# Opening stage of a two-layer diffusion backbone: constant products ahead of the first block, h transferred after the second, transposes and sums at other places

## The chip, the core and the metric

The kernel runs on one core of one Trainium2 chip. The metric is device time in microseconds of one execution, as the median of several. All arithmetic on the tokens is float32 in effect: large products are made of three products in a rounded float32 form, small ones of full float32 products.

## What is computed

The reference is a backbone of two layers over 256 latent and 256 context tokens of 1024 channels. In each layer both token sets pass a half-step gated FFN, then three parallel token mixers (grouped-query attention, differential attention, Fourier mixing) merged by gates, then a second half-step FFN. Every norm is modulated by vectors that come from a conditioning vector:

```python
ml = jnp.split(jax.nn.silu(c) @ w_ada[l] + b_ada[l], N_MOD, axis=-1)
mc = jnp.split(jax.nn.silu(c_ctx)[None] @ w_ada[l] + b_ada[l], N_MOD, axis=-1)
def ffn_half(h, m, k, g_norm, wi, wo):
    hn = modulate(rmsnorm(h, g_norm), m[3 * k], m[3 * k + 1])
    return h + 0.5 * m[3 * k + 2][:, None, :] * swiglu(hn, wi, wo)
```

So the first FFN can start only when three things are there: the first two of nine modulation vectors (shift and scale, 1024 channels each, for c and for c_ctx), the reciprocal root mean square of every token of h, and the first FFN weights.

## The kernel before

**Layout.** Activations lie with channels on the 128 partitions: h is 128 x 8 x 512, eight channel tiles (kt) by 512 tokens (256 latent, 256 context, called the two halves). Weights are held as a high and a low part; a product of activations is three matmuls, `mm3` (lines 309 to 311): high by high, high by low, low by high. The weights come through `WeightStream`: SyncE loads a piece into one of three raw buffers (`wraw`, line 192), ScalarE casts a part of it to the high form (`whi`, line 203), VectorE subtracts to get the low form (`wlo`, line 204), and the next piece is loaded into a raw buffer once both its parts are split.

**The opening, `start`.** The shift and scale of the first norm are made here. Their weights are four blocks `wst[0..3]` of 128 x 8 x 512, 2 MB each: scale and shift of channels 0 to 511 (blocks 0 and 1), then scale and shift of channels 512 to 1023 (blocks 2 and 3). They land in the tiles mg_start, yb_start and, for blocks 2 and 3, two tiles that the profile prints as u_start. SyncE issues everything in written order: `small` (biases, gains, the conditioning vectors), block 0 in five transfers, block 1 in four, with the four transfers of h (512 KB each) between its first and its second half, then blocks 2 and 3, and behind them the first FFN weights.

The steps on the engines, with their lines:

- `dots(i, kts)` (1149): for each channel tile of block i one full float32 product with `scol`, the SiLU of the two conditioning vectors, as stationary operand of two columns and 512 columns of w_ada moving past it. A full float32 product stands in the trace as two MATMUL rows, each with its weight load. The sum over eight channel tiles is copied by ScalarE to `rows` (1151; the profile prints the tile as pt_start).
- `columns(i)` (1157 to 1159): four small transposes turn the two rows into columns, and VectorE adds the bias (line 1159, tile ada).
- squares and sums: ScalarE squares h (1173), VectorE adds the eight channel tiles to one (1171), TensorE sums over the partitions by four products with a column of ones (1186), VectorE takes the reciprocal root (lines 277 to 284) and scales an identity with it (1190), and one product with ones spreads the result over all partitions: r (1195).
- `apply(hf)`: VectorE makes acol, the gain by one plus scale (374); then for each channel tile and half it scales h by acol and r (386), ScalarE adds the shift and rounds to the high part (389), and VectorE makes the low part (390). `apply(0)` covers channel tiles 0 to 3, `apply(1)` 4 to 7. Line 386 needs acol, so the block of scales; lines 389 and 390 need the block of shifts.

Behind `start` comes `cond_region`: GpSimd copies one element of acol (322) as a marker, and behind it loads the conditioning vectors once more, 1 MB (323), for the other modulation vectors, which VectorE forms by multiply and sum during the FFNs (lines 326, 327, 356), with w_ada loaded by GpSimd. The first FFN (`first_pair`) opens with channel tiles 0 to 3 for four accumulators, then tiles 4 to 7.

**What sets the order.** Each engine's order of instructions is settled when the program is built, from the order of the text and from when an operand is reckoned to be ready; so a later step can stand ahead of an earlier one that is not ready. Inside `manual_schedule` for TensorE the matmuls of `start` keep their written order among themselves. In the trace of before, four matmuls of the first FFN stand ahead of the transposes of `columns(3)`.

Of the kernel before, what the change touches and what calls it, by code (L numbers as in the profile page):

```python
# [18 lines left out]
P = 128  # L19
D = 1024  # L20
KT = 8
# [27 lines left out]
def _half(half):  # L49
    return slice(half * 256, half * 256 + 256)  # L50
# [55 lines left out]
class Interleave:  # L106
# [9 lines left out]
    def add(self, q, task, gen=None):  # L116
        if gen is not None:
            task.gen = gen
        self.queues[q].append(task)
        return task  # L120

    def start(self, task, gen):
        task.gen = gen
        self.queues[0].append(task)
        self.step(task)
# [95 lines left out]
class Net:  # L221
# [898 lines left out]
    def start(self):  # L1120

        nc, io = self.nc, self.io
        ccol = self.ccol
        scol = self.pool.tile([P, KT, 2], F32, name="scol")
        nc.sync.dma_start(self.small, io["small"])
        self.h = self.region("h", F32, "start")
        rows = self.region("pt", F32, "start")
        chunks = []
        for i, tag in enumerate(("mg", "yb", "u0", "u1")):
            t = self.region(tag, F32, "start")  # L1130
            for a, b in (((0, 1), (1, 2), (2, 4), (4, 6), (6, 8)) if i == 0 else ((0, 2), (2, 4), (4, 6), (6, 8))):
                nc.sync.dma_start(t[:, a:b, :], io["wst"][i][:, a:b, :])
                if (i, b) == (1, 4):
                    for x in range(4):
                        nc.sync.dma_start(self.h[:, 2 * x:2 * x + 2, :], io["h"][:, 2 * x:2 * x + 2, :])
            chunks.append(t)
        nc.scalar.activation(scol, ccol, AF.Tanh, scale=0.5)
        nc.vector.scalar_tensor_tensor(scol, scol, 1.0, ccol, op0=ALU.add, op1=ALU.mult)
        nc.vector.tensor_scalar(scol, scol, 0.5, None, op0=ALU.mult)
        make_identity(nc, self.ident)  # L1140
        nc.vector.memset(self.ones, 1.0)

        ps = {}

        def dots(i, kts):
            if kts[0] == 0:
                ps[i] = self.mm.next()
            for kt in kts:
                nc.tensor.matmul(ps[i][:2, :], scol[:, kt, :], chunks[i][:, kt, :], start=kt == 0, stop=kt == KT - 1)  # L1149
            if kts[-1] == KT - 1:  # L1150
                nc.scalar.copy(rows[:2, i, :], ps[i][:2, :])

        def columns(i):
            mod, hf = 1 - i % 2, i // 2
            pc = self.mm.next()
            for x in range(4):
                nc.tensor.transpose(pc[:, 2 * x:2 * x + 2], rows[:2, i, x * P:x * P + P], self.ident[:2, :2])
            a = mod * KT + 4 * hf
            nc.vector.tensor_tensor(self.ada[0][:, a:a + 4, :], pc[:, 0:8].rearrange("p (a c) -> p a c", c=2),
                                    self.bada[:, 0, a:a + 4].unsqueeze(2).to_broadcast([P, 4, 2]), op=ALU.add)  # L1160

        def apply(hf):
            ks = slice(4 * hf, 4 * hf + 4)
            self.norm_scale(0, 0, 2, ks)
            for kt in range(ks.start, ks.stop):
                for half in range(2):
                    self.norm_apply(0, 0, kt, half, r[:, _half(half)])

        sq = self.region("ya", F32, "squares")
        two = [sq[:, 2 * i:2 * i + 2, :] for i in range(4)]  # L1170
        add = lambda y, x: nc.vector.tensor_tensor(y, y, x, op=ALU.add)
        for i in range(4):
            nc.scalar.activation(two[i], self.h[:, 2 * i:2 * i + 2, :], AF.Square)
        for y, x in ((0, 1), (2, 3), (0, 2)):
            add(two[y], two[x])
        add(sq[:, 0, :], sq[:, 1, :])
        dg = self.e1.next()
        with self.tc.manual_schedule(engines={mybir.EngineType.PE}):
            dots(0, range(8))
            dots(1, (0, 1))  # L1180
            columns(0)
            dots(1, range(2, 8))
            dots(2, (0,))
            bank = self.att.next()
            for i in range(4):
                nc.tensor.matmul(bank[:, i:i + 1], sq[:, 0, i * P:i * P + P], self.ones[:, 0:1], start=True, stop=True)
            x, y, z = (self.sm.next()[:, 0:4] for _ in range(3))
            self.rsqrt(y, x, bank[:, 0:4], D, z)
            for i in range(4):
                nc.vector.tensor_scalar(dg[:, i * P:i * P + P], self.ident, y[:, i:i + 1], None, op0=ALU.mult)  # L1190
            dots(2, (1,))
            columns(1)
            dots(2, (2, 3, 4))
            r = self.att.next()
            nc.tensor.matmul(r, self.ones, dg, start=True, stop=True)
            apply(0)
            dots(2, (5, 6, 7))
            dots(3, (0, 1))
            columns(2)
            nc.vector.tensor_copy(self.identr, self.ident)  # L1200
            dots(3, range(2, 8))
            columns(3)
            apply(1)
# [141 lines left out]
```

## Time and profile before

| | us |
|---|---|
| median of three runs | 2100.65 |
| lowest and highest | 2099.33, 2103.11 |
| profiled execution | 2100.76 |
| its span, first to last instruction | 2098.7 |
| TensorE matmul busy | 2075.1 (99%) |
| VectorE busy | 1489.6 (71%) |
| ScalarE busy | 920.0 (44%) |
| GpSimd busy | 114.5 (5%) |

The profiled execution is one run; the rows further down are of that run, with times in microseconds from the start of its span. Engines are PE (TensorE matmuls), PEld (its weight loads, which overlap), DVE (VectorE), ACT (ScalarE), POOL (GpSimd) and SP (SyncE, which issues transfers). A busy share is an average over stages; the opening is about 40 of 2100 us. A matmul's printed duration is longer than the distance to the next one, since matmuls overlap at their ends; for what a stretch costs, read the distance between starts.

### The profile page before, as it was taken

The numbers are of one execution on the slowest core, as the hardware profiler recorded it, in microseconds if no ns is written. First come the engines' busy times: TensorE is split into PE (matmuls) and PEld (weight loads), VectorE is DVE, ScalarE is ACT, GpSimd is POOL, SyncE is SP. The second block draws the span as 40 slices with busy tenths as digits, with TensorE's granted clock in tenths as the row PEclk, the third lists the DMA queues.
The fourth block names the chain that finished last, engine by engine and source line by source line (L and its number), as shares of the span: only waits on it lengthen the run. The fifth ranks groups of instructions, "written<-read, shape, count | busy, mean of one in ns | idle before, by whom it ended". The sixth has DMA issues, their size and how long they took to land.

```text
span 2098.7 us, 31520 instructions
## 1 busy us (share of the span) xinstructions
PE 2075.1 (99%) x11640; PEld 1807.9 (86%) x11640; DVE 1489.6 (71%) x3113; ACT 920.0 (44%) x1905; POOL 114.5 (5%) x235
## 2 busy tenths in 40 slices
PE   8999999999999999999999999999999999999999
PEld 3888888899989988988888898888888899999999
DVE  5878776667878865776666668766556688889764
ACT  3323333356765543433333333233334576656553
POOL 2000001100000110000000001000010000000000
PEclk9999999999999999999999999999999999999999
DMA  7645555322222242244444425555553323355665
GB/s 274 229 158 197 174 171 176 98 86 64 70 71 71 86 161 91 74 169 150 153 148 148 143 73 201 181 187 162 179 166 109 96 91 113 122 179 175 197 186 147
DMA packets 86937, 300.47 MB, mean 143 GB/s; under 512 B 10112, under 2 KB 11264, under 8 KB 86528
## 3 DMA queue, kind: packets, MB, share of 16 engines
q1 hardware_dynamic: 64800, 219.29, 32.1%
q0 software_dynamic: 21984, 79.18, 12.1%
q8 instruction: 91, 1.49, 0.3%
q14 instruction: 62, 0.51, 0.1%
HBM read 293.19 MB, written 5.24 MB: 142 GB/s over the span
## 4 chain that ended last, share of the span: by engine, by line
PE 94%; DVE 3%; DMA 2%; ACT 1%; issue 1%; SPq 0%; ACTq 0%; DVEq 0%
PE mm L309 29%; PE mm L311 28%; PE mm L310 28%; PE att L734 1%; PE att L768 1%; PE att L749 1%; DVE wlo L204 1%; PE att L750 1%; PE att L792 1%; PE mm L1149 1%; PE att L311 1%; PE att L310 1%; PE att L309 1%; PE att L303 0%; DMA yb_start<-in_wst 0%
## 5 line engine op out<-in xcount | busy, mean ns | idle before, releaser
L203 ACT CAST whi<-wraw 128x512 fp32r<-128x512 f32 (+2 forms) x840 | 497.9, 596 | 871.1 <-PE mm L310 768.7
L204 DVE TENSOR_TENSOR wlo<-wraw,whi 128x512 fp32r<-128x512 f32 (+2 forms) x840 | 548.8, 658 | 327.5 <-ACT whi L203 323.1
L309 PE MATMUL mm<-hn,whi 128*128 128x512 f32 (+1 forms) x1808 | 641.1, 356 | 1.1 <-ACT hn L389 0.9
L310 PE MATMUL mm<-hn,whi 128*128 128x512 f32 (+1 forms) x1808 | 635.9, 353 | 0.0
L311 PE MATMUL mm<-hn,wlo 128*128 128x512 f32 (+1 forms) x1808 | 635.8, 353 | 0.1
L311 PEld LDWEIGHTS mm<-hn,wlo 128*128 128x128 f32 x1808 | 339.4, 188 | 51.4 <-DVE wlo L204 0.5
L309 PEld LDWEIGHTS mm<-hn,whi 128*128 128x128 f32 x1808 | 339.0, 188 | 49.3 <-issue 1.2
L310 PEld LDWEIGHTS mm<-hn,whi 128*128 128x128 f32 x1808 | 339.3, 188 | 47.4 <-DVE hn L390 0.2
L309 PE MATMUL mm<-whi,hn 128*128 128x384 f32 (+3 forms) x432 | 146.7, 340 | 1.7 <-DVE mg_m L953 1.7
L311 PE MATMUL mm<-whi,hn 128*128 128x384 f32 (+3 forms) x432 | 143.6, 332 | 0.0
L310 PE MATMUL mm<-wlo,hn 128*128 128x384 f32 (+3 forms) x432 | 143.6, 332 | 0.0
L356 DVE CUSTOM_DVE_ANT_0 gt<-ya_c,small 128x1024 bf16<-128x1024 f32 x112 | 141.6, 1280 | 1.7 <-DMA ya_c<-in_wada 1.7
L356 DVE CUSTOM_DVE_ANT_0 e<-ya_c,small 128x1024 bf16<-128x1024 f32 x112 | 141.6, 1280 | 0.0
L352 POOL DMA_DIRECT2D ya_c<-in_wada x128 | 68.1, 532 | 910.9 <-DVE ada L356 882.8
L309 PE MATMUL mm<-u_f,whi 128*128 128x256 f32 (+1 forms) x304 | 101.9, 335 | 0.0
L311 PE MATMUL mm<-u_f,wlo 128*128 128x256 f32 (+1 forms) x304 | 100.9, 332 | 0.0
L310 PE MATMUL mm<-u_f,whi 128*128 128x256 f32 (+1 forms) x304 | 100.9, 332 | 0.0
L438 DVE SCALAR_TENSOR_TENSOR h_h<-mm,gcol,h_h 128x256 f32<-128x256 f32 x104 | 49.9, 482 | 59.9 <-PE mm L311 59.3
L309 PEld LDWEIGHTS mm<-whi,hn 128*128 128x128 f32 x432 | 82.2, 190 | 4.9 <-DVE mg_m L953 2.3
L310 PEld LDWEIGHTS mm<-wlo,hn 128*128 128x128 f32 x432 | 82.3, 191 | 2.5
L311 PEld LDWEIGHTS mm<-whi,hn 128*128 128x128 f32 x432 | 81.9, 190 | 2.7 <-DVE hn L390 0.5
L309 PE MATMUL mm<-mg_f,whi 128*128 128x512 f32 (+1 forms) x204 | 72.1, 353 | 0.0
(288 smaller groups left out, 3284.6 us busy)
## 6 DMA issues: line engine op xcount, KB each, us to landing
wraw<-in_wi SPq DMA_DIRECT2D x172, 512.0 KB, 4.2
ya_c<-in_wada POOLq DMA_DIRECT2D x128, 512.0 KB, 4.0
wraw<-in_wo SPq DMA_DIRECT2D x64, 512.0 KB, 3.7
wraw<-in_gate SPq DMA_DIRECT2D x48, 512.0 KB, 3.6
wraw<-in_win SPq DMA_DIRECT2D x48, 384.0 KB, 3.1
wraw<-in_wo SPq DMA_DIRECT2D x32, 384.0 KB, 3.4
wraw<-in_wbr SPq DMA_DIRECT2D x24, 512.0 KB, 3.5
wraw<-in_wout SPq DMA_DIRECT2D x16, 512.0 KB, 3.6
```

Of the source, the lines that this page charges most:

```text
L203: self.nc.scalar.copy(hi, raw)
L204: self.nc.vector.tensor_tensor(lo, raw, _r(hi), op=ALU.subtract)
L309: mm(out, lh, rh, start=first, stop=False)
L310: mm(out, lh, rl, start=False, stop=False)
L311: mm(out, ll, rh, start=False, stop=last)
L352: self.nc.gpsimd.dma_start(self.adaraw[(self.bg_base + j) % 2], self.io["wada"][l, n])
L356: self.tc.keep_in_program_order(self.nc.vector.tensor_tensor_reduce(self.ft.next().bitcast(BF16), self.adaraw[self.bg_base % 2], self.sil[ ...
L438: self.nc.vector.scalar_tensor_tensor(self.h[:, m, c], ps[:, c], g[:, m, half:half + 1], self.h[:, m, c], op0=ALU.mult, op1=ALU.add)
L734: nc.tensor.matmul(b[:, i * P:i * P + P], src, self.identr, start=True, stop=True)
L749: nc.tensor.matmul(d, qt, k, start=True, stop=False)
L750: nc.tensor.matmul(d, qt, low, start=False, stop=True)
L768: nc.tensor.transpose(ps[:, x * 256 + i * P:x * 256 + i * P + P], es[i][:, k * P:k * P + P], self.ident)
```

## The change

All of it is in `start`. The memset of `ones` stands first in the text. The four transfers of h are issued behind all four of block 1. Ahead of the first dots, TensorE makes eight products of `ones` with `ones` (128 columns) into an otherwise unused accumulator. Among the dots, `columns(0)` follows four channel tiles of block 1 where it followed two; the column sums and the reciprocal root follow four channel tiles of block 2 and `columns(1)` where they followed one channel tile of block 2; `columns(1)` follows four channel tiles of block 2 where it followed two; the spreading product and `apply(0)` follow the whole of block 2 where they followed five channel tiles of it. What stands behind them is unchanged.

```diff
--- before.py
+++ after.py
@@ -1122,6 +1122,7 @@
         nc, io = self.nc, self.io
         ccol = self.ccol
         scol = self.pool.tile([P, KT, 2], F32, name="scol")
+        nc.vector.memset(self.ones, 1.0)
         nc.sync.dma_start(self.small, io["small"])
         self.h = self.region("h", F32, "start")
         rows = self.region("pt", F32, "start")
@@ -1130,7 +1131,7 @@
             t = self.region(tag, F32, "start")
             for a, b in (((0, 1), (1, 2), (2, 4), (4, 6), (6, 8)) if i == 0 else ((0, 2), (2, 4), (4, 6), (6, 8))):
                 nc.sync.dma_start(t[:, a:b, :], io["wst"][i][:, a:b, :])
-                if (i, b) == (1, 4):
+                if (i, b) == (1, KT):
                     for x in range(4):
                         nc.sync.dma_start(self.h[:, 2 * x:2 * x + 2, :], io["h"][:, 2 * x:2 * x + 2, :])
             chunks.append(t)
@@ -1138,7 +1139,6 @@
         nc.vector.scalar_tensor_tensor(scol, scol, 1.0, ccol, op0=ALU.add, op1=ALU.mult)
         nc.vector.tensor_scalar(scol, scol, 0.5, None, op0=ALU.mult)
         make_identity(nc, self.ident)
-        nc.vector.memset(self.ones, 1.0)
 
         ps = {}
 
@@ -1175,12 +1175,17 @@
             add(two[y], two[x])
         add(sq[:, 0, :], sq[:, 1, :])
         dg = self.e1.next()
+        warm = self.att.next()
         with self.tc.manual_schedule(engines={mybir.EngineType.PE}):
+
+            for i in range(8):
+                nc.tensor.matmul(warm[:, 0:P], self.ones, self.ones, start=True, stop=True)
             dots(0, range(8))
-            dots(1, (0, 1))
+            dots(1, range(4))
             columns(0)
-            dots(1, range(2, 8))
-            dots(2, (0,))
+            dots(1, range(4, 8))
+            dots(2, range(4))
+            columns(1)
             bank = self.att.next()
             for i in range(4):
                 nc.tensor.matmul(bank[:, i:i + 1], sq[:, 0, i * P:i * P + P], self.ones[:, 0:1], start=True, stop=True)
@@ -1188,13 +1193,10 @@
             self.rsqrt(y, x, bank[:, 0:4], D, z)
             for i in range(4):
                 nc.vector.tensor_scalar(dg[:, i * P:i * P + P], self.ident, y[:, i:i + 1], None, op0=ALU.mult)
-            dots(2, (1,))
-            columns(1)
-            dots(2, (2, 3, 4))
+            dots(2, range(4, 8))
             r = self.att.next()
             nc.tensor.matmul(r, self.ones, dg, start=True, stop=True)
             apply(0)
-            dots(2, (5, 6, 7))
             dots(3, (0, 1))
             columns(2)
             nc.vector.tensor_copy(self.identr, self.ident)
```

## Rows read from the trace of the kernel before

**Rows 1.** The page, busy time: each engine's us, share of the span, instructions.

```profile
PE 2075.1 (99%) x11640; PEld 1807.9 (86%) x11640; DVE 1489.6 (71%) x3113; ACT 920.0 (44%) x1905; POOL 114.5 (5%) x235
```

**Rows 2.** The chain of waits in order of time, 0 to 62 us: start us, us, what.

```profile
9.53 10.21 DMA yb_start<-in_wst
...
50.34 5.28 DMA wraw<-in_wi
...
59.39 0.51 PE mm L311
```

**Rows 3.** Timeline of TensorE's weight loads: start us, us, engine, line, operation, out<-in, count, idle before.

```profile
8.01 0.13 PEld L1149 LDWEIGHTS mm<-mg_start,scol 128*2 128x2 f32 x1 [0.46 <-issue]
8.86 0.13 PEld L1149 LDWEIGHTS mm<-mg_start,scol 128*2 128x2 f32 x1 [0.72 <-issue]
9.64 0.09 PEld L1149 LDWEIGHTS mm<-mg_start,scol 128*2 128x2 f32 x1 [0.65 <-issue]
10.07 0.09 PEld L1149 LDWEIGHTS mm<-mg_start,scol 128*2 128x2 f32 x1 [0.34 <-issue]
```

**Rows 4.** Windows: stretch, us, busy us (x) of PE, PEld, DVE, ACT, POOL, clock, DMA share, GB/s.

```profile
8.50:9.50 1.00, 1.00 (x2) 0.13 (x1) 0.00 (x0) 0.00 (x0) 0.24 (x2) 1.00 0.99 401
```

**Rows 5.** Timeline of TensorE's products, 0 to 42 us, merged runs, same columns.

```profile
4.64 9.45 PE L1149 MATMUL mm<-mg_start,scol 128*2 128x512 f32 x16 [4.64 <-DMA mg_start<-in_wst]
...
19.79 3.60 PE L1149 MATMUL mm<-yb_start,scol 128*2 128x512 f32 x8 [1.29 <-DMA yb_start<-in_wst]
23.22 1.02 PE L1149 MATMUL mm<-u_start,scol 128*2 128x512 f32 x2
24.17 1.05 PE L1186 MATMUL att<-ones,ya_squares 128*128 128x1 f32 x8
25.15 1.02 PE L1149 MATMUL mm<-u_start,scol 128*2 128x512 f32 x2
...
26.44 2.74 PE L1149 MATMUL mm<-u_start,scol 128*2 128x512 f32 x6
29.11 1.12 PE L1195 MATMUL att<-e,ones 128*128 128x512 f32 x2
30.16 4.45 PE L1149 MATMUL mm<-u_start,scol 128*2 128x512 f32 x10
...
40.12 0.50 PE L309 MATMUL mm<-hn,whi 128*128 128x512 f32 x1
...
40.70 0.39 PE L311 MATMUL mm<-hn,wlo 128*128 128x512 f32 x1
```

**Rows 6.** Timeline of SyncE's queue: the transfers that it issues.

```profile
12.09 9.29 SPq L1132 DMA_DIRECT2D u_start<-in_wst  x8
```

**Rows 7.** Tile u_start (w_ada blocks 2 and 3): its transfers, from issue to landing.

```profile
DMA to landing us min/median/max: 10.2/10.2/10.2
```

**Rows 8.** Timeline of ScalarE: the last square of h.

```profile
18.49 1.06 ACT L1173 ACTIVATE ya_squares<-h_start 128x1024 f32<-128x1024 f32 x1 [0.22 <-DMA h_start<-in_h]
```

**Rows 9.** Timeline of VectorE, 19 to 42 us.

```profile
19.58 3.21 DVE L1171 TENSOR_TENSOR ya_squares<-ya_squares 128x1024 f32<-128x1024 f32 x3 [1.20 <-ACT ya_squares L1173]
25.26 0.16 DVE L277 TENSOR_SCALAR sm<-att 128x4 f32<-128x4 f32 x1 [2.47 <-PE att L1186]
...
27.02 0.88 DVE L1190 TENSOR_SCALAR e<-ident,sm 128x128 f32<-128x128 f32 x4
30.27 0.87 DVE L386 SCALAR_TENSOR_TENSOR gt<-h_start,acol,att 128x256 f32<-128x256 f32 x2 [2.38 <-PE att L1195]
...
38.65 2.09 DVE L204 TENSOR_TENSOR wlo<-wraw,whi 128x256 fp32r<-128x256 f32 x6
41.70 0.17 DVE L1159 TENSOR_TENSOR ada<-mm,small 128x8 f32<-128x8 f32 x1 [0.96 <-PE mm L1157]
```

**Rows 10.** Timeline of GpSimd: the marker that lets the condition vectors' load start.

```profile
36.95 0.26 POOL L322 COPY ya_c<-acol 128x1 f32<-128x1 f32 x1 [23.00 <-ACT whi L203]
```

**Rows 11.** Windows, the stretch in which VectorE waits for the fourth block, columns as in 4.

```profile
38.65:41.70 3.05, 3.05 (x13) 1.27 (x12) 2.09 (x8) 0.58 (x1) 0.00 (x0) 1.00 0.92 290
```

## The prediction

> **What bounds the kernel now.** I read the page first: TensorE is busy 99% of the span [rows 1], so the time can move only where TensorE stands still or runs slowly, and the edit touches nothing behind 45 us. Then the chain of waits over the first 62 us, to see what TensorE waits for there. It runs through a landing of h at 9.53 + 10.21 = 19.74 us (named for the transfer that this landing lets SyncE issue next: the second block's last rows), then through TensorE alone, and around 50 us through a weight load and the VectorE split behind it, until the product of line 311 at 59.39 [rows 2]. So the opening has two kinds of gate: landings up to 20 us, and the weight stream, fed by VectorE, up to 60 us. Third, the weight loads of the first block, for the speed of TensorE: one column product's two halves start 0.85 us apart (8.01 to 8.86), the next 0.78, from 9.64 on 0.43 [rows 3]. The factor of two is that of the clock's two levels, 1.2 and 2.4 GHz; the windows print a granted clock of 1.00 for 8.5 to 9.5 us all the same [rows 4], so I go by the distances. Last, the timelines of the engines, to price each piece.
>
> **Prices.** I call half of one full-precision product a pass. Eight passes of the second block take 23.22 - 19.79 = 3.43 us, 0.429 each [rows 5]. The column sums (eight short passes) cost 25.15 - 23.22 less two passes, 1.07 us. A group of four transposes costs 26.44 - 25.15 less two passes, 0.43. The product that spreads r costs 30.16 - 26.44 less six passes, 1.15 [rows 5]. Check: from the third block's first pass to the first FFN product there are 32 passes (13.73), the sums, two transpose groups, the spread and 0.09 of drain: 16.90, and the trace has 40.12 - 23.22 = 16.90 [rows 5].
>
> **1. Products of constants.** They can begin once the constant is there, near 1 us, and fill the wait until 4.64 [rows 5]. Eight products are 16 passes of 128 columns: a quarter of 0.429, plus a weight load that the sums' row puts at 0.98 / 8 = 0.12 [rows 5], so 0.23 each at the upper level, 0.46 at the lower: 3.7 to 7.4 us, an end between 4.7 and 8.4. The clock rose about 4.9 us behind the first product (4.64 to some 9.55) [rows 3, 5]; if it does so again, it rises near 5.9, the constants end near 7.2, and the 16 passes of the first block, all at 0.429, end near 14.1; at the slow end, 15.3. Before, they ended at 4.64 + 9.45 = 14.1 [rows 5]. So this part moves the end of the first block by nothing or a little backwards, and neither counts, because of the next gate.
>
> The Trainium skill, in TensorE: Matmul & The Clock Gate, section "Why this matters for your kernels", says to warm the engine up with matmuls before what one wants at full speed; by that the slow passes of the first block would be won back whole. The rows have the slow passes too, but a landing between them and the end; that is a rival below.
>
> **2. h behind the whole second block.** No transfer is added; two of w_ada pass four of h in SyncE's queue. The eight transfers of the third and fourth block are issued over 9.29 us, the queue running full, about 1.28 us each [rows 6]; I keep that spacing. The second block's last halves come 4 landings sooner (5.1 us) and h two later (2.6 us). Everything behind them keeps its place: the third block's first rows are issued at 12.09 and land 10.2 us later, at 22.3 [rows 6, 7]. The wait at 19.79 goes; what is late next is this landing. TensorE, done with the first block at 14.1 to 15.3, needs 16 passes and one transpose group, 7.3 us, and comes to the third block at 21.4 to 22.6. It starts at about 22.38 instead of 23.22: **0.84 us** gained of the 2 to 3 that the clock and the wait would offer. At the slow end of part 1, 0.6.
>
> **3. Sums later.** The last square of h begins at 18.49, held by h [rows 8]; 2.6 later it ends at 22.1, and VectorE's adds, 3.21 us behind it [rows 9], end near 25.3. The sums' new place, behind eight passes and columns(1), is 22.38 + 3.43 + 0.43 = 26.2. No wait, 0.9 to spare. From the sums' end to the scaled identity VectorE takes 27.90 - 25.26 = 2.6 us [rows 9], and eight passes (3.43) now lie over it. No wait either.
>
> **4. What the later place does to VectorE.** Between the third block's first pass and the end of the spread there were 10 passes; now there are 16. The spread is done at 22.38 + 6.86 + 1.07 + 0.43 + 1.15 = 31.89 instead of 30.16: **1.73 us later**. VectorE waits for it, idle 2.38 us, and then works 8.4 us without a break on the modulated h before the first weight split (30.27 to 38.65) [rows 9]. All that queues behind: the splits, through them the release of the raw buffers and SyncE's next weight loads, and acol, behind which GpSimd's marker holds the condition load [rows 10]. If the order stays, the first low part, some 0.4 us of split, is ready near 38.65 + 0.4 + 1.73 = 40.8. TensorE would come to line 311 at 39.28 + 0.58 = 39.86, so it waits 0.9 us and stands at 40.8 against 40.70 before [rows 5]: the 0.84 is gone at this point.
>
> **5. Transposes of the fourth block.** Their written place is unchanged, but the block ends at 39.28 while VectorE is 1.73 late. VectorE idled 0.96 us in front of line 1159, between the six splits and the fourth block's columns [rows 9, 11]. Now the columns are there by 39.28 + copy and transposes, about 40.4, and the splits end at 40.74 + 1.73: that idle goes. So VectorE comes out of the stretch 1.73 - 0.96 = **0.77 us** late.
>
> **Sum.** The next gate on the chain is the split that line 311 waits for at 59.39, behind a 5.28 us load that starts when a split frees its buffer [rows 2]. It follows VectorE: +0.77. TensorE, there with +0.1, waits for it; behind it TensorE is the bound and carries the delay to the end. Ends for this term: +0.1 if only the first gate counts, +1.73 if none of VectorE's idle is won back (the marker and its load late as well). I take 0.77, since rows 11 show the idle that is removed. The profiled execution took 2100.76 us (span 2098.7); 2101.53 for it. The median is 0.11 lower: **2101.4 us**, own range 2100.7 to 2102.4.
>
> **Rivals.** Engine orders are settled when the program is built, and this trace cannot show the new one.
>
> A. *The clock's gain comes through.* The first block's slow passes cost 5 x 0.42 + 0.35 = 2.5 us over the fast ones. If nothing landed late behind them, 2100.65 - 2.5 = 2098.2. By the skill's rule above, this is the result. Against it: the landing at 22.3 lies behind the first two blocks whatever their speed. Chance 0.06.
>
> B. *VectorE is not the gate.* If the first weights' casts and splits are ordered into VectorE's wait for the spread (its 2.38 us idle is there for it), line 311 does not wait and the 0.84 stays: 2099.8. Against it: in the rows all six splits stand behind the modulated h. Chance 0.24.
>
> C. *Slower: the fourth block overtakes the weights.* Its columns now come near 40.4, about when VectorE reaches its first split (40.4). If line 1159 is ordered in front of the splits, the 12 remaining VectorE operations of the second half of the modulated h can go first: 12 x 0.43 (half of the pair's 0.87) = 5.2 us [rows 9]. The buffers are freed, and SyncE's loads issued, that much later, and the gate at 59.39 moves by 0.77 + 5.2: 2106.6. It counts as slower once eight of the twelve go ahead. Against it: before, the splits stood ahead, and single splits fit between. Chance 0.10.
>
> D. *Another order further on*, in the FFN, of unknown sign: 0.07.
>
> **How the numbers follow.** The forecast has 0.53. Below 0.2%, 4.2 us, about what a measurement here can tell from none, lie the forecast, A and B, 0.83 together. Slower: C and 0.03 of D, 0.13. Faster: 0.04 of D; no case of the opening can give it, since the third block's landing and 16.90 us behind it leave 0.84. The three runs shown spread from 2099.33 to 2103.11, so a median may stand one or two off its place: the range goes from A, 2098.1, to 2104.8, above the forecast's upper end by that, and leaves out C and D.
>
> **What the profile after would show.** Right: constants on TensorE from about 1 us; 0.43 us between the first block's passes; no wait near 19; the third block's first pass at 22.4, waiting for u_start; the spread done near 31.9; the first line 311 near 40.8, held by the split; line 311's wait near 60 held by a split or load, some 0.8 late. Wrong: the third block starting before 22, the spread before 31, splits ahead of the modulated h (B), or line 1159's last one ahead of the splits (C).

## The result, and the profile after

The changed kernel takes 2110.98 us (median of 6 runs, 2107.63 to 2112.14) against 2100.07 for the kernel before (6 runs): ratio 1.0055, 95% interval 1.004 to 1.0069. It is slower by about 11 us; 2101.4 was forecast, with a range up to 2104.8.

All of it lies in the opening. The first store of h, at the end of the first FFN, is a good mark, since the work up to it, apart from the constant products, is the same in every kernel here. The tile view of park has it at 327.8 us before and 338.2 after:

```profile
L1218 POOL DMA_DIRECT2D park<-h_start x16: 542/542/559, 327.8 to 407.7; - x16
```

```profile
L1220 POOL DMA_DIRECT2D park<-h_start x16: 539/539/557, 338.2 to 417.5; - x16
```

That is +10.4, and the profiled spans differ by 2109.3 - 2098.7 = 10.6. Totals of one and the same kernel spread by several us (the kernel before: 2091.89 to 2106.05 over all runs of this study). Much of it lies behind 1600 us: from the last store of the second park group to the end, with the same work, the profile of before has 492.6 us and that of one run below (before, splits behind) 484.8 (from 1606.1 and from 1616.0). So below the mark is read beside the totals.

The chain of waits of the changed kernel, in order of time (start us, us, what), answers to [rows 2]:

```profile
12.90 10.20 DMA u_start<-in_wst
...
23.14 5.29 PE mm L1149 x8
...
42.17 6.69 DMA ya_c<-in_cc
...
50.04 1.23 DVE ya_c L327
...
52.05 1.14 DVE ya_c L327
53.19 0.34 DVE wlo L204
...
53.58 0.80 PE mm L311
```

Two things are new: the chain goes through the condition load (`in_cc`) and the condition products of line 327, and only then through a weight split to line 311. TensorE's timeline, against [rows 5]:

```profile
1.04 3.78 PE L1182 MATMUL att<-ones 128*128 128x128 f32 x16 [1.04 <-DVE ones L1125]
4.75 2.81 PE L1149 MATMUL mm<-mg_start,scol 128*2 128x512 f32 x4
...
17.55 3.59 PE L1149 MATMUL mm<-yb_start,scol 128*2 128x512 f32 x8
23.14 5.29 PE L1149 MATMUL mm<-u_start,scol 128*2 128x512 f32 x8 [2.00 <-DMA u_start<-in_wst]
...
33.21 1.12 PE L1198 MATMUL att<-e,ones 128*128 128x512 f32 x2
...
41.65 0.51 PE L309 MATMUL mm<-hn,whi 128*128 128x512 f32 x1
...
46.23 0.39 PE L310 MATMUL mm<-hn,whi 128*128 128x512 f32 x1
53.58 0.80 PE L311 MATMUL mm<-hn,wlo 128*128 128x512 f32 x1 [6.97 <-DVE wlo L204]
54.17 0.63 PE L309 MATMUL mm<-hn,whi 128*128 128x512 f32 x1
54.60 0.63 PE L310 MATMUL mm<-hn,whi 128*128 128x512 f32 x1
```

The third block is waited for (2.00 us idle), its eight passes take 28.37 - 23.14 = 5.23 us in place of 3.43, the first FFN product comes at 41.65 in place of 40.12, and then TensorE stands still for 6.97 us in the middle of the FFN's first pair, where before it waited 0.28. Behind that the starts lie 0.43 apart instead of 0.23. The windows show both dips of the clock (columns as in [rows 4], the one before the last two is the granted clock):

```profile
20.00:30.00 10.00, 8.01 (x24) 2.23 (x23) 4.71 (x7) 2.81 (x4) 0.00 (x0) 0.83 1.03 409
...
50.00:60.00 10.00, 6.42 (x19) 5.20 (x20) 5.16 (x10) 1.75 (x4) 1.06 (x2) 0.66 0.58 177
```

The sum: +1.53 at the first FFN product, 6.97 - 0.28 = 6.7 of waiting, and some ten products at 0.2 more, 2.0: 10.2 of the 10.4. VectorE's timeline says what the wait is for, against [rows 9]:

```profile
34.37 0.87 DVE L386 SCALAR_TENSOR_TENSOR gt<-h_start,acol,att 128x256 f32<-128x256 f32 x2 [2.13 <-PE att L1198]
...
40.61 0.41 DVE L204 TENSOR_TENSOR wlo<-wraw,whi 128x256 fp32r<-128x256 f32 x1
...
41.41 0.42 DVE L204 TENSOR_TENSOR wlo<-wraw,whi 128x256 fp32r<-128x256 f32 x1
...
43.23 0.17 DVE L1159 TENSOR_TENSOR ada<-mm,small 128x8 f32<-128x8 f32 x1 [1.01 <-PE mm L1157]
...
50.04 1.23 DVE L327 SCALAR_TENSOR_TENSOR ya_c<-ya_c 128x1024 f32<-128x1024 f32 x1 [1.52 <-ACT ya_c L326]
...
53.11 2.10 DVE L204 TENSOR_TENSOR wlo<-wraw,whi 128x256 fp32r<-128x256 f32 x6
```

Before, six splits stood in one row at 38.65 [rows 9]. Now only two stand there, at 40.61 and 41.41; then come the fourth block's columns (line 1159), the rest of the second half of the modulated h, the two condition products, and the other splits at 53.11. They were not waiting for ScalarE, which had cast all six first pieces by 38.8:

```profile
38.43 0.39 ACT L203 CAST whi<-wraw 128x256 fp32r<-128x256 f32 x1
```

GpSimd's marker, 36.95 before [rows 10], follows acol and is late too, and with it the load that line 327 needs:

```profile
41.67 0.20 POOL L322 COPY ya_c<-acol 128x1 f32<-128x1 f32 x1 [27.23 <-DVE acol L374]
```

So the loss looks like rival C with more behind the overtaking than was priced. Two theories went to the chip. **Theory O**: the new places (sums, spread and transposes) turn the order on VectorE, and that is the loss. **Theory T**: constants and early second block bring TensorE too early to the third block; the wait and the fallen clock are the loss. From the fifth run on a third one stands beside them, **theory S**: the later spread as such is the loss.

### The profile page after: what moved, and what is told of

Its sections match the earlier page's. It is cut to its first block, busy times and chain, and to the rows that moved or that the text cites. A ratio compares the mean times of both kernels' runs of the same rounds, so it can differ in the third digit from the quotient of the medians.

```text
span 2109.3 us, 31551 instructions
## 1 busy us (share of the span) xinstructions
PE 2080.3 (99%) x11656; PEld 1811.9 (86%) x11656; DVE 1489.1 (71%) x3113; ACT 920.4 (44%) x1905; POOL 113.8 (5%) x235
## 4 chain that ended last, share of the span: by engine, by line
PE 94%; DVE 3%; DMA 2%; ACT 1%; issue 0%; SPq 0%; POOL 0%; ACTq 0%; POOLq 0%; DVEq 0%
PE mm L309 29%; PE mm L311 29%; PE mm L310 28%; PE att L734 1%; PE att L768 1%; PE att L749 1%; PE att L750 1%; PE att L792 1%; DVE wlo L204 1%; PE att L311 1%; PE att L303 0%; DMA u_start<-in_wst 0%; PE att L309 0%; PE att L310 0%; DMA yb_start<-in_wst 0%
## 5 line engine op out<-in xcount | busy, mean ns | idle before, releaser
L311 PE MATMUL mm<-mg_f,wlo 128*128 128x512 f32 (+1 forms) x204 | 71.8, 352 | 0.0
```

Source lines behind the costliest of these rows:

```text
L311: mm(out, ll, rh, start=False, stop=last)
```

## The experiments

The kernels differ from one another only in order, transfers and constant products. The marks of all of them, read from their profiles (spread: start of the spreading product; wait: TensorE at line 311 for a split; line 267: start of ScalarE's first cast there, in the first FFN; ratio to before with its interval):

| kernel | spread | wait | line 267 | park | ratio |
|---|---|---|---|---|---|
| before | 29.11 | 0.3 | 62.59 | 327.8 | |
| changed | 33.21 | 7.0 | 72.87 | 338.2 | 1.0055 (1.004 to 1.0069) |
| places only | 33.63 | 8.1 | 73.30 | 339.1 | 1.0048 (1.0029 to 1.0068) |
| h only | 34.71 | none | 68.07 | 333.3 | 1.0023 (1.0009 to 1.0037) |
| constants only | 29.76 | none | 62.56 | 328.1 | 1.001 (0.9996 to 1.0024) |
| all but constants | 31.49 | 7.7 | 71.45 | 336.7 | 1.0051 (1.0034 to 1.0068) |
| splits ahead | 31.11 | 2.7 | 65.96 | 331.4 | 1.0018 (1.0004 to 1.0032) |
| spread three earlier | 29.82 | 1.4 | 64.61 | 329.8 | 1.0018 (1.0001 to 1.0035) |
| early condition load | 31.15 | 7.4 | 68.94 | 338.2 | one run, 2112.80 |
| constants in the wait | 31.70 | 7.7 | 71.71 | 338.1 | one run, 2112.01 |
| before, splits behind | 29.99 | 7.6 | 69.87 | 338.0 | 1.0039 (1.0019 to 1.0059) |
| spread one earlier | 30.73 | 5.4 | 70.37 | 335.8 | one run, 2108.07 |
| constants and splits | 29.78 | 1.6 | 65.05 | 330.2 | 1.0013 (0.9998 to 1.0027) |

### The parts one by one

**Places only.** The kernel before with the changed list of dots, columns, sums and spread:

```diff
             dots(0, range(8))
-            dots(1, (0, 1))
+            dots(1, range(4))
             columns(0)
-            dots(1, range(2, 8))
-            dots(2, (0,))
+            dots(1, range(4, 8))
+            dots(2, range(4))
+            columns(1)
...
-            dots(2, (1,))
-            columns(1)
-            dots(2, (2, 3, 4))
+            dots(2, range(4, 8))
             r = self.att.next()
...
-            dots(2, (5, 6, 7))
```

> Before, with the new places of transposes, sums and spread alone (no constant products, h where it was). Theory O (order on VectorE: with these places four of the first six weight splits stand behind the products of the condition vectors, which wait for a 1 MB load, and TensorE waits for the splits): most of the loss is here, +7 to +10 us, ratio 1.0035 to 1.005; the first FFN stands still for 5 to 7 us near 47 to 53 us, and some passes behind it run at the lower clock. Theory T (the loss comes from TensorE waiting for the third block at 23 us with its clock falling, brought by constants and h together): no such wait here, 0 to +2 us.

Park is at 339.1, +11.3, ratio 1.0048. The whole loss is here, with h and the constants as before. VectorE and the waits of that run:

```profile
41.82 0.42 DVE L204 TENSOR_TENSOR wlo<-wraw,whi 128x256 fp32r<-128x256 f32 x1
...
54.67 2.10 DVE L204 TENSOR_TENSOR wlo<-wraw,whi 128x256 fp32r<-128x256 f32 x6
```

```profile
PE mm L311 <- DVE wlo L204: 8.1, 1, 8.1
```

The splits part in the same place as in the changed kernel. Theory T, which wanted at most 2 us here, falls as the main cause. (The clock fell in this run too, at the second block behind a wait of 1.81 us; what that is worth is told apart further down.)

**h only.**

```diff
-                if (i, b) == (1, 4):
+                if (i, b) == (1, KT):
```

> Before, with h behind the whole second block alone. Theory O: the splits stay ahead of the second half of the modulated h and of the condition products; within 2 us of before (ratio 0.999 to 1.001), the sums waiting for h some 1 us. Theory T: the third block's landing is met earlier, TensorE waits there; +1 to +4 us.

Neither expectation held well. Park is +5.5, more than theory O's 2 us, and the reason is the sums at their old place, not the third block:

```profile
22.68 1.02 PE L1149 MATMUL mm<-u_start,scol 128*2 128x512 f32 x2 [0.97 <-DMA u_start<-in_wst]
26.58 1.51 PE L1186 MATMUL att<-ones,ya_squares 128*128 128x1 f32 x8 [2.88 <-DVE ya_squares L1171]
```

TensorE waits 2.88 us for VectorE's adds, since h is late; the clock falls (0.85 and 0.81 in the windows from 20 to 40 us), and the spread comes at 34.71. So late h does need later sums; the trouble is what the later places do to VectorE. One thing more: the spread is later here than in the changed kernel (34.71 against 33.21), and still six splits stand ahead of the fourth block's columns (two at 41.62 and 42.82, then four), and line 311 does not wait:

```profile
44.72 1.43 DVE L204 TENSOR_TENSOR wlo<-wraw,whi 128x256 fp32r<-128x256 f32 x4
47.31 0.17 DVE L1159 TENSOR_TENSOR ada<-mm,small 128x8 f32<-128x8 f32 x1 [1.16 <-PE mm L1157]
```

So it is the places in the program that turn the order, not a spread that runs late on the chip.

**Constants only.** The memset first in the text, and:

```diff
+        warm = self.att.next()
...
+            for i in range(8):
+                nc.tensor.matmul(warm[:, 0:P], self.ones, self.ones, start=True, stop=True)
```

> Before, with the eight products of constants alone. Theory O: within 2 us of before (0.999 to 1.001): the first block ends up to 1 us earlier and the wait for the second half of block 1 takes that back. Theory T: 0 to +3 us, if the longer wait near 19 us lets the clock fall.

Park 328.1, +0.3, ratio 1.001 with an interval that includes 1; both theories allow it. The first block's passes are at full speed earlier, from 6.91 on. The second block's first half ends earlier and the wait for its second half, 1.29 us before, becomes 2.78:

```profile
6.91 1.02 PE L1149 MATMUL mm<-mg_start,scol 128*2 128x512 f32 x2 [0.75 <-DMA mg_start<-in_wst]
...
15.78 1.88 PE L1149 MATMUL mm<-yb_start,scol 128*2 128x512 f32 x4
20.44 3.60 PE L1149 MATMUL mm<-yb_start,scol 128*2 128x512 f32 x8 [2.78 <-DMA yb_start<-in_wst]
```

**All but constants.** The changed kernel without those lines.

> The changed kernel without the constant products. Theory O: as the changed kernel, +8 to +11 us against before (ratio 1.004 to 1.005), since the places are the same; the constants are worth under 1.5 us. Theory T: without constants TensorE comes to the third block later, waits less and keeps its clock: at most +5 us.

Ratio 1.0051, park +8.9. The third block starts at 23.12, as with constants (23.14), and waits the same:

```profile
23.12 3.60 PE L1149 MATMUL mm<-u_start,scol 128*2 128x512 f32 x8 [1.99 <-DMA u_start<-in_wst]
```

The eight passes take 3.52 us here, not 5.23: the wait of 1.99 us did not lower the clock in this run. The constants neither cause the loss nor gain anything that the totals show (1.0051 without, 1.0055 with them): the landing stands between them and the rest.

### The order alone, both ways

**Splits ahead.** The changed kernel, only the first six casts and splits with a higher priority in the builder's ordering:

```diff
...
-            self.nc.scalar.copy(hi, raw)
-            self.nc.vector.tensor_tensor(lo, raw, _r(hi), op=ALU.subtract)
+            with (self.tc.high_priority(offset=50) if self.split < 6 else nullcontext()):
+                self.nc.scalar.copy(hi, raw); self.nc.vector.tensor_tensor(lo, raw, _r(hi), op=ALU.subtract)
```

> The changed kernel, every place as it is, with the first six weight casts and splits given a higher priority, so that on VectorE all six stand ahead of the second half of the modulated h. Yardstick in all runs: the first cast of line 267 on ScalarE, 62.59 us before, 72.87 in the changed kernel. Theory O (the order of VectorE is the loss): 63.5 to 66.5, the wait of line 311 gone; in total +1 to +4 us against before (ratio 1.0005 to 1.002). Theory S (the later spread as such, some 4 us, and the clock that falls in front of it): still 69 or more.

Line 267 at 65.96, park +3.6 in place of +10.4. VectorE:

```profile
38.51 0.42 DVE L204 TENSOR_TENSOR wlo<-wraw,whi 128x256 fp32r<-128x256 f32 x1
...
39.24 1.76 DVE L204 TENSOR_TENSOR wlo<-wraw,whi 128x256 fp32r<-128x256 f32 x5
...
53.62 1.76 DVE L204 TENSOR_TENSOR wlo<-wraw,whi 128x256 fp32r<-128x256 f32 x5
```

The six splits are done by 41. What is left, 2.7 us of wait, is for the next splits, which stand behind the condition products: "the wait of line 311 gone" was too much. The clock did not fall at the third block in this run, so its spread is 2.1 us earlier than the changed kernel's, and part of the gain could be that. The fair neighbour is all but constants, whose clock held too and whose spread stands at 31.49 against 31.11 here: park 336.7 against 331.4. The order is worth some 5 us in that pair.

**Spread three products earlier.** The changed kernel with

```diff
-            dots(2, range(4, 8))
+            dots(2, range(4, 5))
             r = self.att.next()
...
             apply(0)
+            dots(2, range(5, 8))
```

> The changed kernel with the spread and apply(0) three products earlier (behind channel tile 4 of block 2, as before), all else as changed. The order on VectorE is then again that of before, six splits ahead of the second half. Theory O: yardstick 63 to 66.5, total +1 to +4 us. Theory S: the spread is at most 2.6 us earlier, so the yardstick is 70 or more.

Park 329.8, +2.0, ratio 1.0018 (1.0001 to 1.0035). All six splits are again ahead of the fourth block's columns, two at 36.73 and 37.97 and four in a row:

```profile
39.87 1.43 DVE L204 TENSOR_TENSOR wlo<-wraw,whi 128x256 fp32r<-128x256 f32 x4
42.41 0.17 DVE L1159 TENSOR_TENSOR ada<-mm,small 128x8 f32<-128x8 f32 x1 [1.11 <-PE mm L1157]
```

The spread begins 3.39 us earlier than in the changed kernel, and 8.4 us come back at park: more than its lateness (of which 0.8 is an earlier landing of the third block), against theory S.

**Before, splits behind.** The converse: the kernel before with every place, transfer and product as it was, and only

```diff
...
-            self.nc.vector.tensor_tensor(lo, raw, _r(hi), op=ALU.subtract)
+            s = self.nc.vector.tensor_tensor(lo, raw, _r(hi), op=ALU.subtract); s = self.tc.keep_in_program_order(s) if self.split < 6 else s
```

> The kernel before, every place, transfer and product as it was; only the first six weight splits are pinned on VectorE behind what stands ahead of them in the text, so behind the second half of the modulated h and the condition products. Second yardstick, from here on the better one: the first store of h at the end of the first FFN (tile park), 327.8 us before, 338.2 in the changed kernel. Theory O: the order alone makes the loss: line 311 waits 5 to 8 us, park at 334 to 339, total +6 to +11 us (ratio 1.003 to 1.005). If the order needs the later spread to cost anything: park at most 331, total within 3 us.

```profile
49.20 1.22 DVE L327 SCALAR_TENSOR_TENSOR ya_c<-ya_c 128x1024 f32<-128x1024 f32 x1
50.33 2.09 DVE L204 TENSOR_TENSOR wlo<-wraw,whi 128x256 fp32r<-128x256 f32 x6
```

```profile
PE mm L311 <- DVE wlo L204: 7.6, 1, 7.6
```

Park 338.0, +10.2, of which 0.9 is a later third block in that run (24.10 against 23.22). With the spread where it was, the order alone costs 9.3 us: a loss of the changed kernel's size. It is not quite its order: here all six splits stand behind the condition products, in the changed kernel four do, and here those products do not wait for their load. At the earlier mark, line 267, this run is at +7.3 where the changed kernel is at +10.3. Theory O is shown from both sides: such an order makes the loss by itself, and with the splits ahead most of the loss is gone.

### What in the order costs, and how it turns

**Early condition load.** The changed kernel with

```diff
-        self.cond_region("c0", self.acol[:, KT - 1, 0:1])
+        self.cond_region("c0", self.acol[:, 0, 0:1])
```

> The changed kernel with the marker for the condition load on the first element of acol, so that the load starts some 10 us earlier and its products no longer hold VectorE; the splits then all stand behind the second half of the modulated h. If the wait for the load is what the splits lose: the line 311 wait shrinks by 4 us or more, yardstick 65 to 69. If standing behind the second half of the modulated h is enough: splits near 50, yardstick 69 to 72, total +7 to +10 us.

The load is issued at 28.32 in place of 42.17, and line 327 no longer waits for it. Park is still 338.2. Line 267 came at 68.94, inside the range of "the load is what counts", but its other half, a wait smaller by 4 us, failed (7.4 against 7.0), and since park did not follow it, the early cast was probably a different order of TensorE's products. The splits:

```profile
48.97 1.22 DVE L327 SCALAR_TENSOR_TENSOR ya_c<-ya_c 128x1024 f32<-128x1024 f32 x1
...
50.89 2.10 DVE L204 TENSOR_TENSOR wlo<-wraw,whi 128x256 fp32r<-128x256 f32 x6
```

Standing behind the second half of the modulated h and the two products is enough for such a loss, even without the wait for the load. What that wait is worth in the changed kernel this single run does not tell: all six splits are behind now, and ScalarE does the early condition products ahead of its casts, for which TensorE waits as well:

```profile
42.26 0.50 PE L309 MATMUL mm<-hn,whi 128*128 128x512 f32 x1 [1.69 <-ACT whi L203]
```


**Constants in the wait.** The changed kernel with five more constant products behind the second block:

```diff
             dots(1, range(4, 8))
+            for i in range(5):
+                nc.tensor.matmul(warm[:, 0:P], self.ones, self.ones, start=True, stop=True)
```

> The changed kernel with five more constant products behind the second block, where TensorE waits 2 us or more for the third. If the idle wait is what lets the clock fall there: the third block's eight passes take 3.4 to 3.7 us instead of 5.23, the spread ends 1 to 1.8 us earlier. Theory O: the yardstick gains no more than that (71 to 73), since the order on VectorE is unchanged; total still +7 us or more. Theory S: it gains more, 69 or less.

```profile
21.30 1.38 PE L1188 MATMUL att<-ones 128*128 128x128 f32 x10
23.29 3.60 PE L1149 MATMUL mm<-u_start,scol 128*2 128x512 f32 x8 [0.60 <-DMA u_start<-in_wst]
```

The eight passes run at full speed and the spread comes 1.5 us earlier than in the changed kernel; park stays at 338.1. That the filled wait kept the clock up is not shown, since it held behind an unfilled 1.99 us as well (all but constants). What the dip costs is: of the 1.5 us, 0.76 is left where line 311 starts (52.82 against 53.58), since VectorE still holds the splits, and the passes at the lower clock behind that wait, two more here, take nearly all of the rest. In this one run the dip at the third block is worth nothing at park.

**Spread one product earlier.** As three earlier, with `range(4, 7)` ahead of the spread and channel tile 7 behind.

> The changed kernel with the spread and apply(0) one product earlier. The order on VectorE has then three of six splits ahead of the second half of the modulated h, three behind the condition products (changed kernel: two and four). Theory O: little is won, park at 335 to 338.5. If the loss grew evenly with the lateness of the spread, a third of what three products gave back (8.4 us at park) would come back: 335.4 or less.

Park 335.8: inside theory O's range and 0.4 above the other bound (its third block came 0.8 us later than in the run with three). A third split now stands ahead of the condition products, though behind the fourth block's columns; the others follow behind:

```profile
42.08 0.42 DVE L204 TENSOR_TENSOR wlo<-wraw,whi 128x256 fp32r<-128x256 f32 x1
...
51.14 1.76 DVE L204 TENSOR_TENSOR wlo<-wraw,whi 128x256 fp32r<-128x256 f32 x5
```

This run alone can't tell an even growth from a jump.

**Constants and splits.** The kernel before with the constant products and the priority for six splits.

> The kernel before with the constant products and with the first six splits at higher priority, h and all places as before: the two pieces that the runs so far leave as harmless or useful. Theory O: park at 326.5 to 328.5, total within 1.5 us of before; the landings near 20 us hold the opening, so no gain that can be measured.

A miss: park 330.2, +2.4. The splits now push acol back (39.62, before 36.61), so the condition load comes later and the next splits wait for line 327:

```profile
39.62 0.16 DVE L374 SCALAR_TENSOR_TENSOR acol<-ada,small 128x8 f32<-128x8 f32 x1
...
52.97 1.42 DVE L204 TENSOR_TENSOR wlo<-wraw,whi 128x256 fp32r<-128x256 f32 x4
```

No version here beats the kernel before.

## Why the prediction was wrong

- **Constants (part 1): harmless, as forecast, but the price was wrong.** They ended at 4.75, the early end of 4.7 to 8.4 (the forecast went on with 7.2), and the 16 passes took 0.23 us each, the figure priced for the upper level. But they stood at the lower one: the four passes behind them still take 2.81 us, 0.70 each and not 0.43, and in the run with constants in the wait, at the upper level, ten such passes take 1.38 us, under 0.14 each. That the price for the upper level met the time at the lower one is luck. The first block ended at 13.7 (14.1 to 15.3 forecast), and at 13.7 without constants too (all but constants): its own rows land late, with a wait of 0.98 us up to 8.54. Rival A, the gain of the clock carried to the end, did not happen. The Trainium skill's advice to warm the engine up first (TensorE: Matmul & The Clock Gate, "Why this matters for your kernels") agrees with the trace on the clock: with constants only the passes are at full speed from 6.91 on, before from 9.64 on [rows 3] (8.52 in all but constants). No run shows a gain in time from it.
- **Landing (part 2): the mechanism right, the size off.** The third block is what TensorE waits for, at 23.10 instead of 22.3: its transfer takes the 10.2 us of the forecast, but was issued at 12.90 and not at 12.09. Runs with the same queue order had the first pass between 22.3 and 23.3. A wait of up to 1 us follows from the forecast's own times (21.4 against 22.4); it was 2.00, and that the clock could fall there was not foreseen: 1.8 us. Together the spread began 2.5 us later than the forecast's 30.74 (31.89 less 1.15). In the one run with constants in the wait the clock's part of it did not matter. One reading ahead of it was wrong and changed nothing: the piece from 9.53 to 19.74 [rows 2] is the transfer of the second block's own rows, for which the pass at 19.79 waits [rows 5], not a landing of h.
- **Sums (part 3): no wait, as forecast, but with nothing to spare.** The adds end at 26.9 (25.3 forecast), the sums begin at 28.70 without a wait, and so does the spread. The slow passes had made room: in the run with splits ahead, where the clock held, the adds end at 26.54 and the sums begin at 26.60.
- **VectorE (parts 4 and 5): here it failed.** "If the order stays" was the condition, and it did not stay. Rival C reckoned that the fourth block's columns and the first split would come at about the same time (both near 40.4); part 5 nevertheless counted the vanished idle in front of line 1159 as a gain of 0.96. The forecast had line 311 waiting 0.9 us for its first split and about 0.8 at the later gate. The first line 311 ran at 42.23 without a wait; then four of the first six splits stood behind the columns, the second half of the modulated h and the condition products, and TensorE waited 6.97 us. How the builder came to turn the order no trace shows; that the places turned it, the runs do.
- **Rival C had the place and the sign, 0.10 of chance and about half the price.** It counted twelve operations ahead of the splits, 5.2 us, and 2106.6 in all. The mark moved by 10.4: the condition products stood in front too (2.4 us), a wait for their load, the later spread, and the clock that fell in TensorE's wait (2.0 us). With nothing but the order turned, in the kernel before, it was 9.3.
- **Had the order stayed,** the run with the spread three products earlier says what the opening would have cost: +2.0 at park, where +0.77 was forecast. The first FFN product is 0.7 late there (40.83 against 40.12), and line 311 waits 1.38 us for a split at 61.36 in place of 0.28, which makes 1.8. In front of its spread stands a wait of 1.60 us for the scaled identity, which the changed kernel does not have.

## What to carry to other kernels

Where an engine's order is settled by readiness at build time, a move on one engine can turn the order on another; list the instructions of the fullest engine around the move and ask which pairs come near to changing places, and price the whole queue that would then stand in front. A near tie in one's own sum is a warning and not a gain. And a gain in front of a landing was worth nothing in these runs: find the next landing first.

## What the runs showed of the hardware

Behind a wait of about 2 us TensorE's clock fell in some runs and held in others. In these profiles the waits of 2.00 us (the changed kernel) and 1.81 us (places only, second block's second half) were followed by passes at the lower level, 5.1 to 5.2 us for eight; those of 1.99, 1.91, 1.93, 1.81 and even 2.78 us (all but constants, splits ahead, spread three earlier, early condition load, constants only) by passes at 0.43. The length of the wait alone does not decide it.

The same queue landed its rows at slightly different times from run to run: the third block's first pass stood at 22.33 with the spread three products earlier and at 23.14 in the changed kernel, with the same transfers in the same order. The block's own transfer took 10.2 us in both; it was issued at 12.06 and at 12.90, each time as a transfer of the second block landed (3.69 + 8.36 and 3.54 + 9.34). An opening that hangs on a landing should be read over several profiles.
